# Pads in four SBUF pools of a hybrid streaming layer, and source order for its first twelve weight blocks

## The chip, the cores and the metric

The kernel runs on one core of one Trainium2 chip. The metric is the device time of one execution in microseconds (us); the median of the runs is what a change is judged by. On the core, TensorE does the matrix products into PSUM, VectorE (DVE), ScalarE (ACT) and GpSimd (POOL) do the work on vectors, SyncE (SP) issues most of the DMAs, and the DMA engines move data between HBM and SBUF. SBUF is the working memory: 128 partitions, and a tile takes the same range of bytes in each of them.

## The reference, cut to what matters

One layer of a streaming encoder over 384 tokens: 256 of a new prompt and 8 x 16 of running streams. All data is float32.

```python
h    = rmsnorm(x, norm_mix_g)                       # 384 x 2048
proj = h @ w_in                                     # columns: GLU | q | k | v | forget | gate A | gate B
u    = glu_in[..., :1024] * sigmoid(glu_in[..., 1024:])
z    = layernorm(causal_dwconv(concat(conv_buf, u), conv_dw_w, conv_dw_b), conv_ln_g, conv_ln_b)
a_out = (z * sigmoid(z)) @ conv_pw_out              # 1024 -> 2048
q, k = rmsnorm(q, q_norm_g), rmsnorm(k, k_norm_g)
logf = log_sigmoid(f_logit + b_forget)
b_out = attention(q, k, v, logf) @ w_att_out        # 1024 -> 2048
x    = x + (sigmoid(gA) * a_out + sigmoid(gB) * b_out) @ w_out
h2   = rmsnorm(x, norm_ffn_g)
up   = h2 @ w_up                                    # 2048 -> 2 x 5632
gc   = causal_dwconv(concat(ffn_buf, up[..., :5632]), ffn_dw_w, ffn_dw_b)
x    = x + (silu(gc) * up[..., 5632:]) @ w_down     # 5632 -> 2048
```

The kernel returns the two outputs x, the new keys, values and forget logits, and the last rows of both convolutions' inputs.

## The kernel before, in words

**Products.** Every float32 factor is split into a high part, rounded to the matrix engine's faster format, and a low part, the rest. A product is a trio of matmuls, one line of code each: high x high, high x low, low x high. Operands have 128 rows. In a job of kind "B" (lines 579 to 581, in the FFN lines 1807 to 1809) the *stationary* operand, which is loaded into the array ahead of the matmul, is a 128 x 128 piece of activations, and the *moving* one is a row of 512 (for V 344) weight columns. In a job of kind "A" (lines 574 to 576, the GLU columns) it is the other way round: the stationary operand is a piece of a weight tile, the moving one 384 tokens. The function `seven` (lines 618 to 620) does the Q columns with sums of tokens as further stationary operands (tiles `xsum0` to `xsum3`).

**Stages in the order of TensorE.** V columns, then Q, K, the rest of V, GLU columns beside the attention, gates A and B, then the attention's output projection (stationary tiles `aHL0`, `aHL1`) interleaved with the convolution's pointwise one (`zt0`, `zt1`), `w_out` (`mix0` to `mix3`), and the FFN (`xg`, `sums`, `late`, `x21h`/`x21l`, `act`). TensorE's instructions run in the order of the source.

**Weights.** The list `plan` holds all weight blocks of the kernel in the order of use; a block is 256 rows by 344 or 512 columns. `ahead` takes the next block off `plan` and calls `operand`: `fetch` issues its DMA on SP into one of three `raw` tiles, `split_rows` makes `hi` (ACT, line 408) and `lo` (DVE, line 409) in one of three pairs of tiles. So the load of a block waits until the `lo` of the third block before it is done. The first 16 blocks, here called b0 to b15, are those of V.

**x at the start.** `load_x` loads x by chunks of 128 features (lines 343 and 345, two DMAs for a chunk or a pair of them). `x_chunk` turns a chunk with three transposes on TensorE (line 696) and makes its high and low parts in the tiles `hT` (ACT line 700, DVE line 701). The generator `first_norm` calls it for chunks 2 to 15 between the V products and squares x for the norm on ACT (line 845). In the source, chunks 0 to 3 come first with b0 and b1, then pairs: 4 and 5 ahead of b3, 6 and 7 ahead of b5, and so on to 14 and 15 ahead of b13. `x_sums` and `token_sums` (lines 713 to 729) make `xsum` on ACT and DVE.

**What orders the queues.** The kernel is built three times. The first two builds give a class `Planner` the dependences, the places of the tiles and a cost for each instruction; it schedules greedily, always the ready instruction with the earliest due time on the engine that is free first, and the third build ties every instruction of ACT, DVE, SP and POOL ahead of the FFN to its predecessor in that schedule. A few rules are fixed in it: TensorE's order, the opening up to b1 (lines 734 to 764), the order of `log["chain"]`. The function `queued` marks an instruction as one of a chain in the order of the source on its engine. Before the change it puts the links of the chain into `log["chain"]` only where `banks` is filled, and that is in the FFN.

**Pools and places.** Tiles lie in pools that are stacked from both ends of the partition. From the left: `hi_lo` (3 `hi`, 3 `lo`, 4096 bytes each), `acts` (4 tiles of 12288 bytes), and on top of these, one after another, `x0` (x), `pair`, `convs`, `convs` with `attHL` on it, and `xg`. From the right, among others: `qkv`, and below it first `sums`, later `att`. Starts of the tiles from which stationary operands are read, in bytes of a partition, as the allocation of the kernel before has them:

| tiles | pool | first start | start modulo 128 | start modulo 512 |
|---|---|---|---|---|
| `hi`, `lo` (moving; stationary in GLU) | hi_lo | 2176 | 0 | 128 |
| `hT`, `mix`, `act`, `late` | acts | 26752 | 0 | 128 |
| `xsum0` | sums | 113760 | 96 | 96 |
| `hi`, `lo` of every fourth GLU block | att | 128992 | 96 | 480 |
| `aHL0` | attHL | 100704 | 96 | 352 |
| `zt0` | attHL | 125280 | 96 | 352 |
| `xg0`, `x21h`, `sums0` | xg | 75904, 116864, 125056 | 0 | 128 |

Each piece of such a tile that is loaded starts a multiple of 512 bytes further on.

Of the kernel before, what the change touches and what calls it, by code (L numbers as in the profile page):

```python
# [8 lines left out]
F32 = mybir.dt.float32  # L9
# [6 lines left out]
P = 128  # L16
# [18 lines left out]
TURN_AHEAD, PAIR_AHEAD = 100, 100  # L35
LAST_SUMS, SQ_WAIT = 8, 0

R_FFN, R_DWB, R_LNG, R_LNB, R_FDB, R_QG, R_N = 0, 16, 24, 32, 40, 84, 85
WARM, FILL = 5, 2

# [209 lines left out]
def hybrid_step(  # L250
# [12 lines left out]
    def pool(name, side="left", bufs=1, space=None):  # L263
        kw = dict(name=name, bufs=bufs, reuse_waits="tile")
        if space is not None:
            kw["space"] = space
        else:
            kw["side"] = side
        cm = tc.tile_pool(**kw)
        p = cm.__enter__()  # L270
        return p, lambda: cm.__exit__(None, None, None)

    cp, close_cp = pool("consts", side="right")
    rp, close_rp = pool("raw", side="right")
    wp, close_wp = pool("hi_lo")
    gp, close_gp = pool("acts")
    bank_pool, close_banks = pool("banks", space=PSUM)

    made = [-1, -1]
    banks, free = [], []  # L280
# [37 lines left out]
    xs = [p_x0.tile([P, NTT, 512], F32, name=f"xs{n}") for n in range(4)]  # L318
    xin = [x_prompt[0, 0:P, :], x_prompt[0, P:2 * P, :], x_sample.rearrange("b t d -> (b t) d")]

    newest = {}

    def kept(d):
        if order is None:
# [2 lines left out]
    def behind(ins, name):  # L327
        tc.add_manual_dep(ins, name, mybir.DependencyInfo(
            mybir.DependencyClass.NoSync, mybir.DependencyReason.DATA), reason="queue")

    def queued(d, chain=True):
        e = d.ins.engine
        if chain and e in newest:
            if banks or order is None:
                behind(d.ins, newest[e])
            if banks:
                log["chain"].append((newest[e], d.ins.name))
        newest[e] = d.ins.name

    def load_x(c, n):  # L340
        cs = slice(c * P, (c + n) * P)
        o = c % 4 * P
        queued(nc.sync.dma_start(xs[c // 4][:, 0:2, o:o + n * P],
                                 x_prompt[0, :, cs].rearrange("(t p) d -> p t d", p=P)))
        queued(nc.sync.dma_start(xs[c // 4][:, 2, o:o + n * P], xin[2][:, cs]))


    ident = cp.tile([P, P], F32, name="ident")
    nc.gpsimd.memset(ident[:], 0.0)
    queued(nc.gpsimd.affine_select(out=ident[:], in_=ident[:], pattern=[[-1, P]], compare_op=ALU.not_equal, fill=1.0,  # L350
                                   base=0, channel_multiplier=1))

# [60 lines left out]
        split_rows(hi, lo, raw, o, slice(0, 2))  # L413
        return hi, lo

    plan = []

    def planned(w, k0, cols, nk, *more):
        for k in range(k0, k0 + nk, 2):
# [62 lines left out]
    v_last = len(plan) - 16  # L482
# [192 lines left out]
    def drain(g):  # L675
        for _ in g:
            pass

    def job(kind, nk, act, evac, n=512, done=None):
        d = dict(kind=kind, nk=nk, act=act, evac=evac, n=n)  # L680
        if done is not None:
            d["done"] = done
        return d
# [101 lines left out]
    qt = p_qkv.tile([P, NTT, 1024], F32, name="qt")  # L785
    p_sm, close_sm = pool("sums", side="right")
    sums = [p_sm.tile([P, 2, 5, 2, P], F32R, tag=f"xsum{n}", bufs=1, name=f"xsum{n}") for n in range(4)]
    vrow = p_qkv.tile([P, P], F32, name="vrow")
    rows = [(norm_ffn_g, R_FFN, 16), (conv_dw_b, R_DWB, 8), (conv_ln_g, R_LNG, 8),
            (conv_ln_b, R_LNB, 8), (ffn_dw_b, R_FDB, 44), (q_norm_g, R_QG, 1)]  # L790
# [243 lines left out]
    p_cs, close_cs = pool("convs")  # L1034
# [3 lines left out]
    p_att, close_att = pool("att", side="right")  # L1038
# [141 lines left out]
    def glu_evac(g):  # L1180
        def ev(m, ps):
            if m < 2:
                sgb[m] = p_att.tile([P, NT], F32, tag="sgb", bufs=2, name="sgb")
                tt(sgb[m][:], ps[:, :NT], rs1b[:], op=ALU.mult)
                nc.scalar.activation(sgb[m][:], sgb[m][:], AF.Sigmoid)
            else:
                u = ut[:, 2 * g + m - 2, :]
                tt(u, ps[:, :NT], rs1b[:], op=ALU.mult)
                nc.gpsimd.tensor_tensor(u, u, sgb[m - 2][:], op=ALU.mult)
        return ev  # L1190

    sm = p_cs.tile([P, NT], F32, name="sm")
    sc = p_cs.tile([P, 8, 32], F32, name="sc")
    nc.gpsimd.memset(sc[:], 0.0)

    def conv():
        exts = {}
# [60 lines left out]
    att_steps = attention()  # L1258
    gemm([job("A", 16, ha, glu_evac(g)) for g in range(4)], [att_steps, conv_steps])
    drain(att_steps)  # L1260
    close_att()
    close_qkv()

# [826 lines left out]
```

## Time and profile before

| | |
|---|---|
| median of 3 runs | 1938.84 us (1938.63 to 1939.09) |
| the profiled execution | 1937.07 us, its span 1935.4 us |
| busy: TensorE, its weight loads | 1925.9 us, 1623.6 us |
| busy: DVE, ACT, POOL | 1609.7, 957.2, 153.2 us |
| granted TensorE clock | 1.000 |
| DMA | 293.37 MB, mean 152 GB/s |

The span runs from the first instruction of the program to the end of the last; the execution's own time has the launch around it. "Busy" is time in which at least one instruction of the engine is under way. Matmuls overlap each other, so a row's duration is not what a matmul adds to the time: that is the distance between the starts of neighbouring rows. A timeline lists instructions in the order of start: start, duration, engine, line, operation, output and inputs, shape, count, and in brackets the idle time ahead of it with what ended it. SPq is SyncE's queue, where a duration is the time that the DMA instruction took to be issued, waits included.

### The profile page before, as it was taken

The page shows a single profiled execution, that of the slowest core. Times are in us where ns is not written, and L with a number is a line of the kernel's source. Part 1 is how long each engine was busy: PE and PEld are TensorE (multiplying, and loading weights), DVE is VectorE, ACT ScalarE, POOL GpSimd, SP SyncE. Part 2 cuts the span into 40 slices and gives each one's busy share as a digit, 9 for nine tenths or more (in the row PEclk, how much of TensorE's full clock was granted, in tenths as well). Part 3 has the DMA queues.
Part 4 walks back from the last instruction along what each step waited for, and adds up shares of the span by engine and source line. Part 5 has one row for each costly group of instructions (what it writes and reads, how often), then busy time and mean ns, then how long its engine had stood idle before and what let it go on. Part 6 is the DMA issues. An engine that isn't in the chain of part 4 may idle for free.

```text
span 1935.4 us, 25489 instructions
## 1 busy us (share of the span) xinstructions
PE 1925.9 (100%) x9108; PEld 1623.6 (84%) x9108; DVE 1609.7 (83%) x2213; ACT 957.2 (49%) x1355; POOL 153.2 (8%) x298
## 2 busy tenths in 40 slices
PE   9999999999999999999999999999999999999999
PEld 8888999988888888888888888888888888888887
DVE  6878879998764568687699989899999999999985
ACT  7564444433333522354555464555555555555552
POOL 1000011100000000000101010101010101101010
PEclk9999999999999999999999999999999999999999
DMA  6547776344444333744545454545454545545453
GB/s 199 153 139 162 229 189 159 107 143 129 133 133 129 122 124 127 201 133 130 148 147 164 148 164 148 152 153 162 133 164 150 167 156 150 162 143 176 131 171 133
DMA packets 220722, 293.37 MB, mean 152 GB/s; under 512 B 59355, under 2 KB 105110, under 8 KB 220588
## 3 DMA queue, kind: packets, MB, share of 16 engines
q1 hardware_dynamic: 213395, 281.74, 49.0%
q0 software_dynamic: 7168, 10.00, 2.0%
q8 instruction: 71, 1.16, 0.2%
q14 instruction: 56, 0.45, 0.1%
q10 hardware_dynamic: 32, 0.01, 0.0%
HBM read 266.98 MB, written 7.86 MB: 142 GB/s over the span
## 4 chain that ended last, share of the span: by engine, by line
PE 98%; DMA 1%; ACT 0%; SPq 0%; DVE 0%; issue 0%; ACTq 0%
PE bank L1807 18%; PE bank L1808 18%; PE bank L1809 18%; PE bank L579 11%; PE bank L581 11%; PE bank L580 11%; PE bank L574 2%; PE bank L576 2%; PE bank L575 2%; PE bank L620 1%; PE bank L619 1%; PE bank L618 1%; DMA xs<-in_x_prompt_dram 1%; PE bank L1106 0%; PE bank L1147 0%; PE bank L1127 0%
## 5 line engine op out<-in xcount | busy, mean ns | idle before, releaser
L408 ACT CAST hi<-raw 128x1024 fp32r<-128x1024 f32 (+2 forms) x227 | 229.9, 1016 | 407.5 <-PE bank L581 256.1
L1499 ACT CAST hi<-raw 128x1024 fp32r<-128x1024 f32 x260 | 270.5, 1052 | 315.9 <-DVE raw L1499 140.2
L409 DVE TENSOR_TENSOR lo<-raw,hi 128x1024 fp32r<-128x1024 f32 (+2 forms) x227 | 268.1, 1184 | 158.6 <-ACT hi L408 157.0
L1499 DVE TENSOR_TENSOR lo<-raw,hi 128x1024 fp32r<-128x1024 f32 x260 | 314.1, 1218 | 49.0 <-ACT hi L1499 47.2
L579 PE MATMUL bank<-hi,hT 128*128 128x512 f32 (+1 forms) x624 | 235.6, 377 | 1.5 <-ACT hT L700 1.0
L580 PE MATMUL bank<-lo,hT 128*128 128x512 f32 (+1 forms) x624 | 232.8, 373 | 0.8 <-DVE lo L409 0.8
L581 PE MATMUL bank<-hi,hT 128*128 128x512 f32 (+1 forms) x624 | 233.3, 374 | 0.1
L1807 PE MATMUL bank<-hi,xg 128*128 128x512 f32 x440 | 171.2, 389 | 0.0
L1808 PE MATMUL bank<-lo,xg 128*128 128x512 f32 x440 | 171.2, 389 | 0.0
L1809 PE MATMUL bank<-hi,xg 128*128 128x512 f32 x440 | 171.2, 389 | 0.0
L1232 DVE SCALAR_TENSOR_TENSOR ut<-ext,cw,ut 128x384 f32<-128x384 f32 x240 | 151.7, 632 | 6.4
L1808 PE MATMUL bank<-lo,act 128*128 128x512 f32 x396 | 154.1, 389 | 0.0
L1809 PE MATMUL bank<-hi,act 128*128 128x512 f32 x396 | 154.0, 389 | 0.0
L1807 PE MATMUL bank<-hi,act 128*128 128x512 f32 x396 | 154.0, 389 | 0.0
L1499 ACT CAST x21h<-raw 128x1024 fp32r<-128x1024 f32 x82 | 86.4, 1054 | 102.9 <-PE bank L1809 52.7
L579 PEld LDWEIGHTS bank<-hi,hT 128*128 128x128 f32 x624 | 117.2, 188 | 21.1 <-ACT hT L700 1.5
L580 PEld LDWEIGHTS bank<-lo,hT 128*128 128x128 f32 x624 | 117.3, 188 | 20.0 <-DVE lo L409 1.3
L581 PEld LDWEIGHTS bank<-hi,hT 128*128 128x128 f32 x624 | 117.1, 188 | 19.9 <-DVE hT L701 0.9
L1499 DVE TENSOR_TENSOR x21l<-raw,x21h 128x1024 fp32r<-128x1024 f32 x82 | 100.2, 1222 | 6.6 <-ACT x21h L1499 5.6
L1809 PEld LDWEIGHTS bank<-hi,xg 128*128 128x128 f32 x440 | 82.6, 188 | 17.2
L1808 PEld LDWEIGHTS bank<-lo,xg 128*128 128x128 f32 x440 | 82.6, 188 | 17.1
L1807 PEld LDWEIGHTS bank<-hi,xg 128*128 128x128 f32 x440 | 82.6, 188 | 17.1
(397 smaller groups left out, 4139.7 us busy)
## 6 DMA issues: line engine op xcount, KB each, us to landing
raw<-in_w_up_dram SPq DMA_DIRECT2D x176, 512.0 KB
raw<-in_w_in_dram SPq DMA_DIRECT2D x96, 512.0 KB
raw<-in_w_down_dram SPq DMA_DIRECT2D x88, 512.0 KB
raw<-in_w_in_dram SPq DMA_DIRECT2D x64, 256.0 KB
raw<-in_w_out_dram SPq DMA_DIRECT2D x32, 512.0 KB
raw<-in_w_att_out_dram SPq DMA_DIRECT2D x16, 512.0 KB
raw<-in_conv_pw_out_dram SPq DMA_DIRECT2D x16, 512.0 KB
raw<-in_w_in_dram SPq DMA_DIRECT2D x23, 344.0 KB
```

Of the source, the lines that this page charges most:

```text
L408: queued(nc.scalar.copy(hi[:, k, :o], raw[:, k, :o]), first)
L409: queued(tt(lo[:, k, :o], raw[:, k, :o], f(hi[:, k, :o]), op=ALU.subtract), first)
L574: mm(o, hi[:, kk, s], ah, start=st, stop=False)
L575: mm(o, hi[:, kk, s], al, start=False, stop=False)
L579: mm(o, ah[:, s], hi[:, kk, :n], start=st, stop=False)
L580: mm(o, ah[:, s], lo[:, kk, :n], start=False, stop=False)
L581: mm(o, al[:, s], hi[:, kk, :n], start=False, stop=sp)
L1232: stt(o, v, wc, o, op0=ALU.mult, op1=ALU.add)
L1499: d = op(*args, **kw)
L1807: mm(o, ah, h[:, kk, :], start=start, stop=False, **kw)
L1808: mm(o, ah, l[:, kk, :], start=False, stop=False, **kw)
L1809: mm(o, al, h[:, kk, :], start=False, stop=stop, **kw)
```

## The change

Four small tiles that nothing uses are added: 384 bytes at the start of `hi_lo`, ahead of its other tiles, 96 bytes in `sums`, 32 bytes in `convs`, and 96 bytes in `att`. What lies left of a pad on a stack stays, what is stacked on it moves. With the sizes above the starts become: `hi` 2560, `hT` and `mix` and `act` 27136, `xg0` 76288, `x21h` 117248, `sums0` 125440 (multiples of 512 all); `xsum0` 113664 (a multiple of 512); `aHL0` 101120 and `zt0` 125696 (256 modulo 512); the `att` tiles `hi` 128896 (384 modulo 512). All are multiples of 128. `qkv` does not move: `vt`, stationary in a few attention products, stays at 154720, which is 96 modulo 128.

In `queued` the condition changes. With `plan` now made ahead of it, a link of the chain is made, and told to the planner, while `plan` is still empty, while at most b0 to b11 have been taken off it (`v_last` is its length less 16, and `EARLY` is 4), and in the FFN as before. So in the opening the DMAs of SP (and the splits and `hT` parts on ACT and DVE) that pass through `queued` keep the source's order among themselves up to b11; what does not pass through it there (squares, `x_sums`), and all later work, is placed by the planner.

```diff
+EARLY = 4
 ...
     wp, close_wp = pool("hi_lo")
+    wp.tile([P, 96], F32, name="align")
     gp, close_gp = pool("acts")
 ...
-    newest = {}
+    plan, newest = [], {}
 ...
     def queued(d, chain=True):
         e = d.ins.engine
         if chain and e in newest:
-            if banks or order is None:
+            if banks or not plan or len(plan) >= v_last + EARLY:
                 behind(d.ins, newest[e])
-            if banks:
                 log["chain"].append((newest[e], d.ins.name))
         newest[e] = d.ins.name
 ...
-    plan = []
 ...
     sums = [p_sm.tile([P, 2, 5, 2, P], F32R, tag=f"xsum{n}", bufs=1, name=f"xsum{n}") for n in range(4)]
+    p_sm.tile([P, 24], F32, name="align")
 ...
     nc.gpsimd.memset(sc[:], 0.0)
+    p_cs.tile([P, 8], F32, name="align")
 ...
     drain(att_steps)
+    p_att.tile([P, 24], F32, name="align")
     close_att()
```

## The prediction

> **What bounds the kernel now.** I read the page's busy times and its chain of work first, then the stretches of equal length, then single matmuls in the timeline.
>
> ```profile
> span 1935.4 us, 25489 instructions
> PE 1925.9 (100%) x9108; PEld 1623.6 (84%) x9108; DVE 1609.7 (83%) x2213; ACT 957.2 (49%) x1355; POOL 153.2 (8%) x298
> PE 98%; DMA 1%; ACT 0%; SPq 0%; DVE 0%; issue 0%; ACTq 0%
> ```
>
> TensorE is busy all but 9.5 us of the span, and the chain that ended last is 98% its own instructions. So the time is the number of matmuls times the distance of their starts, plus what little TensorE waits. "Busy" hides both, since overlapping matmuls count as busy whatever their distance. The stretches count matmuls in equal times (columns: stretch, length, then busy time and number for each engine, clock, DMA share, GB/s):
>
> ```profile
> 725.80:774.20 48.40, 48.40 (x209) 38.89 (x208) 41.22 (x58) 14.31 (x16) 0.00 (x0) 1.00 0.38 126
> 1209.60:1258.00 48.40, 48.40 (x215) 40.07 (x214) 42.77 (x56) 29.00 (x41) 9.55 (x19) 1.00 0.51 152
> ```
>
> The first lies mostly in the stage of attention output and pointwise projection, the second in the FFN. Both have trios with 512 moving columns at full clock, and TensorE sits idle in neither; yet one starts 209 in 48.4 us and the other 215. The timeline gives the distance:
>
> ```profile
> 116.18 0.39 PE L618 MATMUL bank<-hi,xsum 128*128 128x512 f32 x1
> 121.55 0.39 PE L620 MATMUL bank<-hi,xsum 128*128 128x512 f32 x1
> ...
> 650.21 0.40 PE L580 MATMUL bank<-lo,aHL 128*128 128x512 f32 x1
> 655.81 0.40 PE L580 MATMUL bank<-lo,aHL 128*128 128x512 f32 x1
> ...
> 1199.98 0.39 PE L1808 MATMUL bank<-x21l,xg 128*128 128x512 f32 x1
> 1205.42 0.39 PE L1808 MATMUL bank<-lo,xg 128*128 128x512 f32 x1
> ```
>
> Between the two rows of `xsum` lie 23 starts: 5.37 / 23 = 0.2335 us. Between those of `aHL` lie 24: 5.60 / 24 = 0.2333. Between those of `xg` lie 24: 5.44 / 24 = 0.2267. So a matmul with `xsum` or `aHL` stationary costs 6.6 ns more than one with `xg`. By the table of places the slow ones start at 96 modulo 128 and the fast one at 0; the region isn't the cause, since `xg`, `x21h` and `sums` lie in the same bytes as `aHL` and `xsum`.
>
> **The change: pads.** Each pad is an unused tile: no instruction and no DMA is added. These rows are of a grouping by line and shape (count, busy, mean ns):
>
> ```profile
> L579 PE MATMUL bank<-hi,aHL 128*128 128x512 f32 x96 | 37.9, 395 | 0.0
> L579 PE MATMUL bank<-hi,zt 128*128 128x512 f32 x96 | 37.9, 395 | 0.0
> L618 PE MATMUL bank<-hi,xsum 128*128 128x512 f32 x40 | 15.8, 394 | 0.0
> ```
>
> Each stands for a trio of three lines, so the slow matmuls are 3 x (96 + 96 + 40) = 696. At 6.6 ns they give back 696 x 0.0066 = 4.6 us: 3.8 in the projections, 0.8 in the Q stage. Nothing lies beside it: TensorE is the path, and what would be late next has room. DVE, which makes the weights' low parts, is busy 41.22 of 48.40 us in the projections' stretch and DMA has a share of 0.38 there; 3% more pace is covered.
>
> GLU has a test of its own: every fourth block there has its stationary weights in `att`, at 96 modulo 128, against 384 moving tokens.
>
> ```profile
> 212.36 0.33 PE L574 MATMUL bank<-hT,hi 128*128 128x384 f32 x1
> 220.71 0.34 PE L574 MATMUL bank<-hT,hi 128*128 128x384 f32 x1
> 224.88 0.35 PE L574 MATMUL bank<-hT,hi 128*128 128x384 f32 x1
> ```
>
> From 212.36 run two blocks at 0 modulo 128, 48 starts, 8.35 / 48 = 0.1740 us; from 220.71 the `att` block, 24 starts, 4.17 / 24 = 0.1738. No difference, so I take nothing for the 7 such blocks of GLU; were they to gain like the others it would be 168 x 6.6 ns = 1.1 us, the upper end. It also warns that I know the cost only where 512 columns move. For the attention's small products in `att` I take nothing either; no row has one of them at both places.
>
> The pad in `hi_lo` is harder. `hT`, `mix`, `act`, `xg` sit at 128 modulo 512 and already run at 0.2267; they move to multiples of 512, where no row of before has a stationary tile. `xsum` (96 modulo 512) and `aHL` (352) cost the same, and so do GLU's two places (128 and 480). In no pair does the place modulo 512 matter, so I take 0, and keep the two other possibilities as rivals.
>
> **The change: order.** The first 57 us hold the only waits of TensorE that are worth anything:
>
> ```profile
> 13.98 0.40 PE L579 MATMUL bank<-hi,hT 128*128 128x344 f32 x1
> ...
> 15.46 0.32 PE L581 MATMUL bank<-hi,hT 128*128 128x344 f32 x1
> 16.17 0.43 PE L579 MATMUL bank<-hi,hT 128*128 128x344 f32 x1 [0.39 <-ACT hT L700]
> ...
> 18.03 0.49 PE L696 MATMUL bank<-ident,xs 128*128 128x128 f32 x3
> 19.01 0.43 PE L579 MATMUL bank<-hi,hT 128*128 128x344 f32 x1 [0.49 <-ACT hi L408]
> 19.92 0.42 PE L580 MATMUL bank<-lo,hT 128*128 128x344 f32 x1 [0.48 <-DVE lo L409]
> ...
> 25.86 0.49 PE L696 MATMUL bank<-ident,xs 128*128 128x128 f32 x3
> 26.11 0.40 PE L579 MATMUL bank<-hi,hT 128*128 128x344 f32 x1
> 26.86 0.42 PE L580 MATMUL bank<-lo,hT 128*128 128x344 f32 x1 [0.34 <-DVE lo L409]
> ...
> 28.86 0.32 PE L581 MATMUL bank<-hi,hT 128*128 128x344 f32 x1
> 32.65 0.32 PE L581 MATMUL bank<-hi,hT 128*128 128x344 f32 x1
> ```
>
> Undisturbed, these start 3.79 / 24 = 0.158 us apart (the last two rows); the restart after a wait costs some 0.1 to 0.4 more. The wait before 16.17 is worth 1.0 us with its restart, those before 19.01 and 19.92 together 1.5 (the block b3), that before 26.86 0.7. Sum 3.2 us. Why, by ACT, DVE and SP's queue:
>
> ```profile
> 9.36 0.88 DVE L409 TENSOR_TENSOR lo<-raw,hi 128x688 fp32r<-128x688 f32 x1 [0.51 <-ACT hi L408]
> ...
> 9.70 0.77 ACT L408 CAST hi<-raw 128x688 fp32r<-128x688 f32 x1
> 14.93 0.63 ACT L845 ACTIVATE junk<-xs 128x512 f32<-128x512 f32 x1 [0.61 <-DMA xs<-in_x_prompt_dram]
> 15.56 0.56 ACT L700 ACTIVATE hT<-bank,gm 128x384 fp32r<-128x384 f32 x1
> 18.19 0.77 ACT L408 CAST hi<-raw 128x688 fp32r<-128x688 f32 x1 [0.99 <-DMA raw<-in_w_in_dram]
> ```
>
> ```profile
> 3.76 0.95 SPq L384 DMA_DIRECT2D raw<-in_w_in_dram  x2
> 4.75 0.47 SPq L343 DMA_DIRECT2D xs<-in_x_prompt_dram  x1
> ...
> 8.61 0.81 SPq L343 DMA_DIRECT2D xs<-in_x_prompt_dram  x1
> 11.77 0.37 SPq L384 DMA_DIRECT2D raw<-in_w_in_dram  x1
> 17.11 0.38 SPq L384 DMA_DIRECT2D raw<-in_w_in_dram  x1
> ```
>
> ```profile
> 12.00:18.00 6.00, 5.55 (x33) 4.66 (x32) 1.57 (x3) 4.56 (x13) 0.00 (x0) 1.00 0.97 353
> 30.00:36.00 6.00, 6.00 (x42) 5.97 (x42) 5.14 (x12) 5.21 (x12) 0.00 (x0) 1.00 0.61 178
> ```
>
> b3 is issued at 11.77 behind the x of chunks 2 to 9, lands only for the `hi` at 18.19, 6.4 us later, in a stretch where the DMA engines are 97% busy: it queues behind x that TensorE doesn't need yet. The `hT` at 15.56 stood behind a square at 14.93 that waited for x.
>
> In the source's order SP runs chunks 2 and 3, b2, chunks 4 and 5, b3, b4, chunks 6 and 7, b5. Of the moved DMAs: b2 goes behind one pair of chunks (256 features x 384 tokens x 4 bytes, 384 KB, 1.1 us at the 353 GB/s of the stretch from 12 us, 2 at half of that; its `hi` ran at 9.70 and its products start at 13.98, so it is covered). Four DMAs of chunks 6 to 9 go behind b3, that is 768 KB out of its way, 2.2 us at 353 GB/s; the planner may put the free pair 14 and 15 into that gap and take half of it back. b3's waits of 1.5 us should go either way, or nearly. b4 waits on SP for `lo` of b1 (9.36 to 10.24) rather than going out at 17.11, and the x of 6 and 7 queues behind that wait: issued near 11, wanted by TensorE at 25.86 (its chunk 6), and even 6.4 us of landing leaves 8. ACT and DVE stand in nearly the source's order already; the squares come later with their x, into 30 to 57, where ACT has room (5.21 of 6.00) and TensorE no wait.
>
> Bounds of this part: +3.2 us if all three waits go; below nothing, a new wait as large as the largest of these, -1.5. I take +1.5, b3's alone: the other two hang on ACT's order, which the planner makes anew. A gain here stays to the end, since after 57 us TensorE has no wait to fill up.
>
> **Sum.** 4.6 + 0 + 1.5 = 6.1 us. The profiled execution took 1937.07 us (span 1935.4 and 1.7 around it), so it would be 1931.0; it lies 1.8 under the median, and on the median of 1938.84 the forecast is 1932.7. Best case of the terms: 4.6 + 1.1 + 3.2 = 8.9, so 1929.9; worst, 4.6 - 1.5 = 3.1, so 1935.7.
>
> **Rivals.**
> - *The place modulo 128 is not what costs.* GLU's blocks speak for it, the two equal rates at 96 modulo 128 against it. Then only the order pays: 1938.84 - 1.5 = 1937.3, no change. [...] Chance 0.07.
> - *The order costs what the pads give.* An x pair or a block lands late behind SP's waits and TensorE loses more than 0.7 us where I expect a gain; with -1.5, 1935.7, no change by the bound below. Chance 0.05.
> - *Slower: a multiple of 512 is a worse place.* If the FFN's tiles took the step of 6.6 ns the wrong way, the 4,900 matmuls after 822 us (1,110 / 0.2267) would lose 32 us: 1965. It decides from 6.1 + 3.9 = 10 us, that is 2 ns each. Nothing speaks for it but that the place is untried. Chance 0.04.
> - *Much faster: a multiple of 512 is a better place.* The same step the right way gives 1938.8 - 6.1 - 32 = 1901. [...] Against it: nothing here varies with the place modulo 512. Chance 0.04.
>
> **How the numbers follow.** The forecast has 0.80. Runs of this kernel agree within 0.03%, but I call faster or slower only what differs by over 0.2%, 3.9 us. Faster: 0.80 and 0.04, 0.84. Same: 0.07 and 0.05, 0.12. Slower: 0.04. The range goes from 1928.8, the best sum with 1.1 more for the attention's products, to 1936.5, past the worst; it leaves out the two rivals of 512, the first rival, and a little of the forecast's tails.
>
> **What would show it.** Right: starts 0.2267 apart for `aHL`, `zt` and `xsum`, the projections' stretch with 215 instead of 209 matmuls, GLU and FFN unchanged; b3 on SP ahead of chunks 6 to 9, no idle time before its matmuls near 18 us. Wrong: 0.2333 again at the new places, another distance in the FFN, or new waits of TensorE on `hT` between 20 and 57 us.

## Result and profile after

| kernel | median | runs | ratio to before, 95% interval |
|---|---|---|---|
| before, timed beside it | 1938.89 us | 9 | |
| after | 1934.51 us | 9 | 0.9976 [0.9966, 0.9986] |

The change is worth 4.4 us, 2.7 to 6.6 by the interval; the lower end of that lies under the 3.9 us from which the prediction calls a change faster. All ratios are taken over undisturbed runs, which leaves out one run of `three_pads` (below) that took 3246.36 us at a granted clock of 0.556. The profiled execution of after took 1935.30 us with a span of 1933.5. The lines of its page that answer to those of before:

```profile
span 1933.5 us, 25489 instructions
PE 1923.6 (99%) x9108; PEld 1627.1 (84%) x9108; DVE 1608.8 (83%) x2213; ACT 956.3 (49%) x1355; POOL 154.5 (8%) x298
PE 99%; SPq 1%; DMA 0%; DVE 0%; issue 0%; ACT 0%
```

The instructions are as many as before, and TensorE is still the whole path; what changed can only be the distance of its starts or its few waits. The same two stretches as before, projections and FFN:

```profile
725.80:774.20 48.40, 48.40 (x215) 40.09 (x214) 42.08 (x60) 13.78 (x16) 0.00 (x0) 1.00 0.39 126
1209.60:1258.00 48.40, 48.40 (x215) 40.10 (x214) 43.67 (x56) 28.30 (x38) 9.58 (x19) 1.00 0.51 150
```

The first went from 209 matmuls to 215; the second kept its 215. DVE is busy 42.08 us of 48.40 in the faster one, so it had the room. The timeline of after, TensorE: the first matmul of Q, of GLU, of the projections and of `w_out`, with pairs of `xsum` and `aHL` between them.

```profile
62.97 0.39 PE L618 MATMUL bank<-hi,hT 128*128 128x512 f32 x1
...
117.42 0.39 PE L618 MATMUL bank<-hi,xsum 128*128 128x512 f32 x1
...
122.63 0.39 PE L620 MATMUL bank<-hi,xsum 128*128 128x512 f32 x1
...
214.18 0.34 PE L574 MATMUL bank<-hT,hi 128*128 128x384 f32 x1
...
643.53 0.39 PE L579 MATMUL bank<-hi,aHL 128*128 128x512 f32 x1
...
649.88 0.39 PE L580 MATMUL bank<-lo,aHL 128*128 128x512 f32 x1
...
655.32 0.39 PE L580 MATMUL bank<-lo,aHL 128*128 128x512 f32 x1
...
774.09 0.39 PE L579 MATMUL bank<-hi,mix 128*128 128x512 f32 x1
```

`aHL`: 5.44 / 24 = 0.2267 us from start to start, where before had 0.2333. `xsum`: 23 starts in 5.21 us, 0.2265. The stages, from these starts and the same ones of before (`w_out` first starts at 775.96 there):

| stage | before, us | after, us | difference |
|---|---|---|---|
| start to first Q | 60.98 | 62.97 | +1.99 |
| Q, K, rest of V | 151.38 | 151.21 | -0.17 |
| GLU, attention, gates | 429.21 | 429.35 | +0.14 |
| projections | 134.39 | 130.56 | -3.83 |
| `w_out`, FFN, to the end | 1159.40 | 1159.42 | +0.02 |

So the projections gave what they were to give, and the opening, where a gain was forecast, is longer. There SP's queue of after shows the order:

```profile
8.32 1.02 SPq L344 DMA_DIRECT2D xs<-in_x_prompt_dram  x1
9.38 0.47 SPq L346 DMA_DIRECT2D xs<-in_x_sample_dram  x1
9.89 0.38 SPq L935 DMA_DIRECT2D cwr<-in_conv_dw_w_dram  x1
10.32 1.48 SPq L938 DMA_DIRECT2D fwr<-in_ffn_dw_w_dram  x1
11.91 1.80 SPq L385 DMA_DIRECT2D raw<-in_w_in_dram  x1
13.75 2.41 SPq L933 DMA_DIRECT2D lp<-in_cache_logf_dram  x1
16.26 0.90 SPq L385 DMA_DIRECT2D raw<-in_w_in_dram  x1
17.21 0.47 SPq L344 DMA_DIRECT2D xs<-in_x_prompt_dram  x1
```

b3 is the `raw` at 11.91, b4 the one at 16.26. Chunks 6 and 7 (17.21) do stand behind b3 now, as the change orders. But ahead of b3 the planner has put x that it was free to move, that of chunks 14 and 15 (8.32, 9.38), and two small loads, `cwr` and `fwr`; `lp` stands ahead of b4. In before, the small loads came after b3 and b4:

```profile
19.04 0.41 SPq L934 DMA_DIRECT2D cwr<-in_conv_dw_w_dram  x1
19.49 0.45 SPq L937 DMA_DIRECT2D fwr<-in_ffn_dw_w_dram  x1
```

So b3 leaves SP no earlier than in before (11.77). Its `hi` runs 7.3 us later, where before had 6.4, and ACT and TensorE wait for it longer:

```profile
19.20 0.76 ACT L409 CAST hi<-raw 128x688 fp32r<-128x688 f32 x1 [2.79 <-DMA raw<-in_w_in_dram]
...
20.02 0.42 PE L579 MATMUL bank<-hi,hT 128*128 128x344 f32 x1 [2.11 <-ACT hi L409]
20.93 0.58 PE L580 MATMUL bank<-lo,hT 128*128 128x344 f32 x1 [0.49 <-DVE lo L410]
21.30 0.49 PE L581 MATMUL bank<-hi,hT 128*128 128x344 f32 x1
...
23.02 0.49 PE L581 MATMUL bank<-hi,hT 128*128 128x344 f32 x1
```

```profile
18.00:24.00 6.00, 3.49 (x13) 3.20 (x14) 2.86 (x5) 3.16 (x6) 0.00 (x0) 0.75 0.92 275
```

The wait for b3 is 2.11 us here against 0.49 in before. Behind it the granted clock was 0.75 over the stretch from 18 us (0.50 from 21.10 to 24.40), and the matmuls of 344 columns there start 1.72 / 6 = 0.287 us apart, where before had 0.158 at a clock of 1.00; these six alone cost 0.8 us more.

### The profile page after: what moved, and what is told of

It reads as the page before. It is cut to its first block, busy times and chain, and to the rows that moved or that the text cites. A ratio compares the mean times of both kernels' runs of the same rounds, so it can differ in the third digit from the quotient of the medians.

```text
span 1933.5 us, 25489 instructions
## 1 busy us (share of the span) xinstructions
PE 1923.6 (99%) x9108; PEld 1627.1 (84%) x9108; DVE 1608.8 (83%) x2213; ACT 956.3 (49%) x1355; POOL 154.5 (8%) x298
## 4 chain that ended last, share of the span: by engine, by line
PE 99%; SPq 1%; DMA 0%; DVE 0%; issue 0%; ACT 0%
PE bank L1811 18%; PE bank L1812 18%; PE bank L1810 18%; PE bank L580 11%; PE bank L579 11%; PE bank L581 11%; PE bank L574 2%; PE bank L576 2%; PE bank L575 2%; PE bank L619 1%; PE bank L620 1%; PE bank L618 1%; DMA raw<-in_w_in_dram 0%; PE bank L1107 0%; PE bank L696 0%; SPq L346 0%
```

## Experiments

Two questions were open: what each half of the change is worth, and whether "a multiple of 128" is what the pads buy. In all kernels the unchanged remainder is as in before or after.

**Each half alone.** `pads_only` is before with the four pads, `order_only` is before with the new condition in `queued` and no pad.

> The four pads on the kernel before, its planned order kept. Theory A (the pads give all of the gain, the order nothing or a loss): 4.6 us less than the kernel before, ratio 0.9976, at least as fast as the changed kernel; aHL, zt and xsum start 0.2267 us apart, the Q products begin near 61.0 us as before. Theory B (the order gives 1.5 us of the gain as forecast, the pads 3.1): ratio 0.9984, slower than the changed kernel by 1.5 us.

> The new condition in queued without any pad. Theory A: 0 to 2 us slower than the kernel before, ratio 1.000 to 1.001; b3 lands near 19 us behind x of chunks 14 and 15 and three small DMAs, TensorE waits 2 us for it, and the Q products begin near 63 us. Theory B: 1.5 us faster, ratio 0.9992, Q products begin near 59.5 us in undisturbed executions.

| kernel | median | ratio to before (1938.98 us) |
|---|---|---|
| pads_only | 1933.21 us | 0.9972 [0.9961, 0.9983] |
| order_only | 1940.15 us | 1.0010 [1.0001, 1.0019] |

The pads alone give 5.8 us by the medians, 3.3 to 7.6 by the interval. The order alone costs 1.2 (0.2 to 3.7). So the whole gain is the pads', and the order takes some of it back. Their stretch in the projections and that of the order alone, pads first:

```profile
725.80:774.20 48.40, 48.40 (x215) 40.10 (x214) 42.07 (x61) 14.23 (x16) 0.00 (x0) 1.00 0.40 131
```

```profile
725.80:774.20 48.40, 48.40 (x209) 38.89 (x208) 40.81 (x58) 13.64 (x16) 0.00 (x0) 1.00 0.39 125
```

And the timeline of `order_only`, ACT and TensorE:

```profile
19.83 0.77 ACT L408 CAST hi<-raw 128x688 fp32r<-128x688 f32 x1 [2.85 <-DMA raw<-in_w_in_dram]
...
20.65 0.42 PE L578 MATMUL bank<-hi,hT 128*128 128x344 f32 x1 [1.89 <-ACT hi L408]
```

The same late b3 as in after, without pads: it belongs to the order. Its granted clock stayed at 1.00 from 18 to 24 us, so the 0.75 of after is not a constant part of that wait.

**More blocks in the source's order.** `early0` is after with all 16 blocks of V, and so the x of chunks 14 and 15 too, in the source's order:

```diff
-EARLY = 4
+EARLY = 0
```

> The changed kernel with EARLY 0: all 16 blocks of V in the source's order, so x of chunks 14 and 15 go behind b12; cwr, fwr and lp still run ahead of b3. Theory A (what is put ahead of b3 is what delays it): 384 KB less ahead of b3, it lands 1 to 1.5 us earlier, near 17.5 to 18 us, TensorE's wait for it falls from 2.1 to under 1 us; 1 to 2 us faster than the changed kernel. Theory C (SP's own waits delay b3, whatever stands ahead): no change.

It took 1934.27 us, ratio 0.9975 [0.9966, 0.9984], no other than after: by the time theory C (SP's own waits) has it, and not theory A with its gain of 1 to 2 us. The rows say more. SP's queue, then ACT and TensorE:

```profile
6.78 0.51 SPq L935 DMA_DIRECT2D cwr<-in_conv_dw_w_dram  x1
7.34 1.24 SPq L938 DMA_DIRECT2D fwr<-in_ffn_dw_w_dram  x1
8.62 0.55 SPq L933 DMA_DIRECT2D lp<-in_cache_logf_dram  x1
9.29 6.19 SPq L385 DMA_DIRECT2D raw<-in_w_in_dram  x2
...
17.44 0.77 ACT L409 CAST hi<-raw 128x688 fp32r<-128x688 f32 x1 [2.74 <-DMA raw<-in_w_in_dram]
...
18.74 0.55 PE L696 MATMUL bank<-ident,xs 128*128 128x128 f32 x3 [1.32 <-ACT qt L713]
```

No x of chunks 14 and 15 stands ahead of b3 any more, but all three small loads do. b3 goes out at 9.29 and its `hi` runs at 17.44 instead of 19.20, about where theory A had it. TensorE still waits 1.32 us, for an ACT instruction that stands behind that `hi`. What is gained there is lost again at Q, where a wait of 1.04 us is new: with `EARLY = 0` the last squares of x are tied to the source's order too, which the next kernel shows.

**The small loads and the last x behind b3.** `late_small` is `early0` with a switch in `queued` that keeps the source's order for `lp`, `cwr` and `fwr` as well:

```diff
-    def queued(d, chain=True):
+    def queued(d, chain=True, late=False):
...
-            if banks or not plan or len(plan) >= v_last + EARLY:
+            if banks or late or not plan or len(plan) >= v_last + EARLY:
```

with `late=True` on the three loads.

> As EARLY 0, and cwr, fwr and lp chained in the source's order too, so that they go out behind the first Q blocks. Theory A: b3 is issued near 9 us, lands near 15, no wait of TensorE for it; Q products begin at 60 us or earlier; 2.5 to 3.5 us faster than the changed kernel, ratio to the kernel before 0.996. Theory C: as the changed kernel.

It took 1931.67 us, ratio 0.9965 [0.9953, 0.9978]. From its timeline:

```profile
8.20 1.66 SPq L385 DMA_DIRECT2D raw<-in_w_in_dram  x2
...
14.88 0.76 ACT L409 CAST hi<-raw 128x688 fp32r<-128x688 f32 x1
...
17.78 0.41 PE L579 MATMUL bank<-hi,hT 128*128 128x344 f32 x1
...
60.77 0.17 DVE L864 COPY rs<-r1r 128x3 f32<-128x3 f32 x1
...
61.05 0.57 DVE L895 TENSOR_SCALAR vt<-bank,rs 128x344 f32<-128x344 f32 x1
61.68 0.50 PE L618 MATMUL bank<-hi,hT 128*128 128x512 f32 x1 [1.03 <-DVE vt L895]
```

b3 goes out at 8.20 with no load ahead of it that isn't wanted first (the small ones follow from 52.85 us), its `hi` runs at 14.88 without a wait, TensorE has none for it at 17.78, and Q starts at 58.40 us instead of 62.97. But part of that is given back at once: the last squares of x run only at 52 to 55 us, the scale `rs` comes at 60.77, V's evacuation to `vt` waits for it, and TensorE waits 1.03 us for the bank. By the time alone `late_small` can't be told from `early0`, as their intervals overlap; that the small loads delay b3 is read from the rows.

**The squares free again.** `sp_only_late` is after (`EARLY` is 4) with `late=True` on the three loads and on both DMAs of `load_x`; SP's order is that of `late_small`, ACT's squares stay with the planner.

> The changed kernel, but the x of all chunks, lp, cwr and fwr always stand in the source's order on SP; ACT's squares keep the planner's order, which the kernel without any reordering of the small loads (the late_small kernel) had chained too. Theory: in late_small the wait of 1.4 us at the start of the Q stage came from the squares of the last group of chunks, chained to a late place on ACT, so that the scale of V's evacuation came late; with the squares free that wait goes and the early gain stays: Q starts near 58.4 us, no wait of TensorE over 0.5 us between 17 and 20 us or between 60 and 63 us, about 1930.4 us, ratio to the kernel before 0.996. Rival: the wait comes from x of chunks 14 and 15 themselves, which stand late on SP: then the wait near 60 us stays and the time is late_small's, 1931.7, ratio 0.9965.

It took 1931.18 us (1930.83 to 1931.45), ratio 0.9961 [0.9947, 0.9974] to a before of 1939.48. Its stretches:

```profile
18.00:24.00 6.00, 6.00 (x41) 5.96 (x40) 3.53 (x7) 5.76 (x12) 0.00 (x0) 1.00 0.77 217
57.00:63.00 6.00, 6.00 (x31) 5.20 (x30) 5.93 (x8) 5.25 (x8) 0.00 (x0) 1.00 0.31 94
```

TensorE is busy throughout in both: 41 matmuls lie between 18 and 24 us where after had 13, and the wait near 61 is gone. The squares run at 41 to 45 us here. Q starts at 58.45. The median is the lowest of all these kernels, 8.3 us (5.0 to 10.3) under before. But its interval overlaps with that of `late_small` and, by 0.0008, that of after, so that it is faster than they are rests on the rows.

**Is a multiple of 128 what counts?** `three_pads` leaves out the 384 bytes of `hi_lo`; `xsum` and the stationary tiles of the projections are at multiples of 128 in it all the same.

> The kernel before with three of the four pads: sums, convs and att, without the 384 bytes of hi_lo. The stationary tiles hT, mix, act, xg stay at 128 modulo 512, while aHL, zt and xsum are at multiples of 128. Theory (only the place modulo 128 counts): the same as all four pads alone, ratio 0.997, 1933 us, all matmuls of 512 columns 0.2267 us apart. Rival (a multiple of 512 is worth something, or hi_lo's pad moved something else): differs from the four pads by more than 2 us, and the FFN's distance is another than 0.2267.

```profile
116.59 0.40 PE L618 MATMUL bank<-hi,xsum 128*128 128x512 f32 x1
121.47 0.40 PE L618 MATMUL bank<-hi,xsum 128*128 128x512 f32 x1
725.80:774.20 48.40, 48.40 (x215) 40.10 (x214) 42.07 (x60) 14.04 (x16) 0.00 (x0) 1.00 0.36 125
```

1935.3 us, ratio 0.9977 [0.9968, 0.9986]: the time can't tell it from the four pads, the rows can. The projections run at 215 as expected. But `xsum`, at 113664, a multiple of 512, takes 21 starts in 4.88 us, 0.2324, and 0.233 on the mean of its matmuls: as slow as in before. So its own place isn't the cause. What differs from after, where the same `xsum` at the same 113664 ran at 0.2267, is the moving tile beside it: `hi` starts at 2176 here, and at 2560 in after. Modulo 256 the two tiles are 128 apart here and 0 apart in after.

**Shifting one side.** `acts_32` and `acts_64` are before with one unused tile of 32 or 64 bytes, so that nearly all stationary tiles move and `hi` and `lo` don't:

```diff
     gp, close_gp = pool("acts")
+    gp.tile([P, 8], F32, name="shift")      # 16 for acts_64
```

> The kernel before with an unused tile of 32 bytes at the start of the pool acts, nothing else. The stationary tiles hT, mix, act, xg, sums, late and x21 go from a multiple of 128 to 32 modulo 128, aHL and zt from 96 to a multiple of 128; xsum stays at 96; the weights' hi and lo keep their places. Theory (a stationary tile that isn't at a multiple of 128 costs 6.6 ns with 512 moving columns): 6,672 matmuls get slower and 576 faster, (6,672 - 576) x 0.0066 = +40 us, 1979 us; FFN starts 0.2333 us apart, aHL and zt 0.2267; V with 344 columns and GLU, whose moving tile hT is shifted here, show whether they pay too (4 us more if V's 432 matmuls and as much if GLU's 768 pay). Rival (something else at the place of xsum and aHL, a partner tile or the size of 96): FFN stays at 0.2267 and the time at 1939 or 1935.

> The kernel before with an unused tile of 64 bytes at the start of the pool acts, nothing else: hT, mix, act, xg, sums, late and x21 at 64 modulo 128, aHL and zt at 32, xsum at 96. If the step is at 64 bytes: FFN stays at 0.2267, aHL and zt at 0.2333, the time at 1939. If the step is at 128 bytes: FFN at 0.2333 too, +44 us, 1983. If the cost grows with the distance from a multiple of 128, FFN lies between or above, and aHL and zt at 32 below or above their 0.2333 at 96.

They took 1973.2 and 1976.3 us, a run each. The two stretches of `acts_32`, then of `acts_64`:

```profile
725.80:774.20 48.40, 48.40 (x215) 40.10 (x214) 37.63 (x53) 14.27 (x16) 0.00 (x0) 1.00 0.37 130
1209.60:1258.00 48.40, 48.40 (x210) 39.20 (x209) 41.69 (x49) 25.49 (x33) 6.91 (x14) 1.00 0.53 162
```

```profile
725.80:774.20 48.40, 48.40 (x209) 38.98 (x208) 36.51 (x51) 13.67 (x16) 0.00 (x0) 1.00 0.36 123
1209.60:1258.00 48.40, 48.40 (x210) 39.03 (x209) 43.52 (x53) 24.97 (x29) 5.63 (x11) 1.00 0.56 179
```

With 32 bytes the projections are cured (209 to 215) and the FFN is made ill (215 to 210). The totals were missed: +34 us in `acts_32` where +40 was expected, +37 in `acts_64` where +44 was expected for a step at 128 bytes. The expectations counted the 1,056 matmuls whose moving tile is `x21h` or `x21l`; those tiles moved by the same bytes as their partner and stayed near 0.2267 (in `acts_32` median 0.227, mean 0.2287). Without them it is (5,616 - 576) x 0.0066 = 33.3 for `acts_32` and 5,616 x 0.0066 = 37.1 for `acts_64`. The sums are thus another sign that the two places count together.

**The two theories against each other.** `all_32` shifts `hi`, `lo` and everything stacked on them by the same 32 bytes; `acts_128` shifts the stationary side by 128, so that each tile that was at a multiple of 128 still is; `sums_224` is `three_pads` with 224 bytes instead of 96 in `sums`, which puts `xsum` a multiple of 256 from `hi`.

```diff
     wp, close_wp = pool("hi_lo")
+    wp.tile([P, 8], F32, name="shift")      # all_32
     gp, close_gp = pool("acts")
+    gp.tile([P, 32], F32, name="shift")     # acts_128
```

> The kernel before with an unused tile of 32 bytes ahead of everything in the pool hi_lo: hi and lo, hT, mix, act, xg, sums, late and x21 all move by the same 32 bytes, to 32 modulo 128; aHL and zt come to a multiple of 128, and xsum stays at 96. Theory (what counts is the distance between the place of the stationary tile and that of the moving one, modulo 256): the FFN's distances are 0 as before, so 0.2267; aHL and zt keep their 224, so 0.2333 although they are at a multiple of 128; time of the kernel before, 1939 us. Rival (what counts is the stationary tile's own place modulo 128): FFN 0.2333 and 5,600 to 6,700 matmuls slower, +37 to +44 us, 1976 to 1983; aHL and zt 0.2267.

> The kernel before with an unused tile of 128 bytes at the start of the pool acts: hT, mix, act, xg, sums and late stay at multiples of 128, but at 128 modulo 256 from the weights' hi and lo. Theory (distance modulo 256): 6,672 matmuls less the 1,056 whose moving tile x21 moves along, 5,616 x 0.0066 = +37 us, 1976 us, FFN 0.2333 with hi and lo, 0.2267 with x21. Rival (a multiple of 128 is enough): no change, 1939 us, FFN 0.2267.

> The three pads of the kernel without hi_lo's pad, but 224 bytes instead of 96 in the pool sums, so that xsum lies a multiple of 256 from hi and lo. Theory (distance modulo 256): xsum 0.2267 instead of 0.2333, 0.8 us less than with 96 bytes, and the time of all four pads, 1933 to 1934 us, ratio 0.997. Rival: xsum stays at 0.2333 because hi_lo's pad brought the gain in another way; time of the three pads, 1935 us, ratio 0.9977.

The stretches of `all_32`, then of `acts_128`, and two rows of `xsum` in `sums_224`:

```profile
725.80:774.20 48.40, 48.40 (x209) 38.91 (x208) 41.21 (x59) 14.32 (x16) 0.00 (x0) 1.00 0.40 130
1209.60:1258.00 48.40, 48.40 (x216) 40.07 (x215) 42.28 (x55) 29.30 (x41) 9.54 (x19) 1.00 0.51 156
```

```profile
725.80:774.20 48.40, 48.40 (x208) 38.90 (x207) 36.35 (x50) 14.23 (x18) 0.00 (x0) 1.00 0.37 120
1209.60:1258.00 48.40, 48.40 (x210) 39.23 (x209) 43.60 (x52) 24.16 (x28) 5.64 (x11) 1.00 0.57 171
```

```profile
117.34 0.39 PE L618 MATMUL bank<-hi,xsum 128*128 128x512 f32 x1
122.10 0.39 PE L618 MATMUL bank<-hi,xsum 128*128 128x512 f32 x1
```

`all_32` took 1937.7 us (one run), the time of before: no FFN tile is at a multiple of 128, and it starts 216; `aHL` and `zt` are at a multiple of 128, and that stretch starts 209. `acts_128` took 1976.5 us (one run): every FFN tile is at a multiple of 128, and it starts 210. In `sums_224` 21 starts of `xsum` take 4.76 us, 0.2267; it took 1934.13 us, ratio 0.9974 [0.9964, 0.9984]. All three went by the distance of the two tiles, none by the stationary tile's own place. Collected, the means of the start-to-start times of the matmuls with 512 moving columns (starts more than 0.26 us apart left out; in the rows of `acts_...` also the 1,056 with `x21h` or `x21l`). The distance is the start of the stationary tile less that of the moving one:

| stationary and moving tile | kernel | distance modulo 256 | mean, us | matmuls |
|---|---|---|---|---|
| FFN and all others with `hi`/`lo` | before | 0 | 0.2268 | 6,619 |
| the same | all_32 | 0 | 0.2268 | 6,619 |
| the same | acts_32 | 32 | 0.2333 | 5,532 |
| the same | acts_64 | 64 | 0.2333 | 5,532 |
| the same | acts_128 | 128 | 0.2331 | 5,530 |
| `aHL`, `zt` | after, three_pads, acts_32 | 0 | 0.2267 | 575 each |
| `aHL`, `zt` | acts_64 | 32 | 0.2333 | 575 |
| `aHL`, `zt` | before, all_32 | 224 | 0.2333 | 575 each |
| `aHL`, `zt` | acts_128 | 96 | 0.2343 | 575 |
| `xsum` | before | 224 | 0.2334 | 103 |
| `xsum` | three_pads | 128 | 0.2331 | 103 |
| `xsum` | all_32 | 192 | 0.2294 | 103 |

Every distance of 0 in the table is fast. `aHL` in after lies 256 from its partner modulo 512 and ran at 0.2267, as fast as the FFN of before at 0 modulo 512 (0.2268). All others are slow; 192 alone lies between, and why isn't known. Distances that aren't a multiple of 32 weren't tried.

## Why the prediction came out, step by step

**The pads' sum** was forecast at 4.6 us, and `pads_only` measured 5.8 (3.3 to 7.6). The projections' 3.8 is exact: 576 matmuls, 134.39 to 130.56 us. The 0.8 in the Q stage is there too: the distances fall from 0.2334 to 0.2267 on 120 matmuls, and from the first Q start to the first of the remaining V matmuls after has 128.49 us where before had 129.30. That the whole stage is only 0.17 us shorter comes from these last 144 matmuls with 344 columns: their starts span 22.56 us in after and 21.93 in before. This isn't the pads' doing, since `early0` with the same pads has 21.93 too and `sums_224` 23.41; what moves it isn't known.

**The step that failed in it** is "the slow ones start at 96 modulo 128 and the fast one at 0", read as the cause. In before the two readings can't be told apart: `hi` and `lo` are at 128 modulo 256, and each fast tile happens to be as well. With this the next step fell too: "In no pair does the place modulo 512 matter, so I take 0" for the pad of `hi_lo`. It is worth the 0.8 us that the sum gave to `sums`, because only together do the two bring `xsum` and `hi` to one place modulo 256 (`three_pads`). The four pads do it all at once, so the total didn't show the error.

**GLU's `att` blocks** were taken at nothing, and the stage shows no gain: 429.21 and 429.35 us. It isn't quite nothing. These blocks lie at a distance of 96 in before, with a mean of 0.1735 from start to start, and at 128 in after, with 0.1759, where after's other blocks, at 0, have 0.1736. In `acts_128` it is the other way round: the blocks at 128 have 0.1758, those of `att`, at 224, 0.1737. So with 384 columns too a distance of 128 costs some 2 ns, and the pads together lose about 168 x 0.0024 = 0.4 us in GLU instead of buying anything. 0 and 96 (before), 32 and 192 (`acts_64`) and 224 (`acts_32`, `acts_128`) all have 0.1734 to 0.1742; 64, the distance of the `att` blocks in `acts_32` and in `all_32`, lies between (0.1745 in one, 0.1755 in the other).

**The order** was forecast at +1.5 us and is -1.2 by `order_only`, inside the bounds and on the wrong side. The step that failed: "Four DMAs of chunks 6 to 9 go behind b3, that is 768 KB out of its way". They did go, but SP's place ahead of b3 didn't stay empty. The working had the planner take half of it back with chunks 14 and 15; it took all of it, with them and with `cwr` and `fwr`, which the working didn't name, although the profile of before has them on the same queue. `late_small` shows it: with these kept behind, b3 leaves at 8.20 and its wait is gone. The three small loads alone count for much of it: with them ahead of b3 and no x, in `early0`, its `hi` ran at 17.44, without them at 14.88. The rival explanation, that b3 is held back by SP's own waits, falls with it: the blocks ahead of b3 are the same there.

**The rivals.** "The order costs what the pads give" came nearer than its chance of 0.05 says: a block did land late, and the order lost more than the 0.7 us that this rival asked for. That the total still fell by over 3.9 us is in part luck: the pads measured 5.8 us and not 4.6, a difference that lies within the noise, and that made up for the 1.2 that the order cost. A forecast of +4.6 for the pads and +1.5 for the order was thus met by the total with the cause of the one misread and the sign of the other wrong. The noise was underrated besides: the 0.03% by which runs agree is from three runs, and the nine of before beside after lie between 1936.93 and 1940.76, 0.2%, as much as the bound for a change. That the place modulo 128 isn't what costs was true, and its consequence, that the pads buy nothing, wasn't. The 32 bytes of `acts_32` cost 34 us, the same 32 bytes on both sides in `all_32` nothing. Both rivals of a multiple of 512 fell: the FFN runs 0.2267 in after as in before. Nor did any placing bring it under 0.2267.

**Opening times in one profile are weak evidence.** With the planner's old order Q started at 60.67 us in `pads_only`, 60.98 in before, 61.29 in `three_pads` and 62.89 in `sums_224`. So of the 1.99 us that the opening lost between the two profiles, only the 1.2 to 1.3 of the medians (`order_only` against before, after against `pads_only`) are put down to the order.

## What to carry to other kernels

Where the same kind of matmul starts at two distances at full clock (0.2267 and 0.2333 us here), compare the places of both its operands, not of the stationary one alone, and move one side, as `acts_32` did by 32 bytes, to see which relation holds before padding everything. Where a planner orders a queue, an order that is fixed for some loads frees slots for the others: list all that is still free to move on that queue, small loads too, and ask what will be set into the gap. And a gain of microseconds in the opening has to be followed to the next stage, where the late scale of V's evacuation took 1.5 us back in `late_small` (Q started as early as in `sp_only_late`, GLU at 210.54 instead of 209.02).

## What was not expected of the hardware

In these kernels a matmul with 512 moving float32r columns cost 0.2267 to 0.2268 us where its stationary and its moving tile lay at a distance of 0 modulo 256 bytes in the partition, and 0.2331 to 0.2334 at distances of 32, 64, 128 and 224, 0.2343 at 96 (0.2294 at 192, `xsum` of `all_32`): 3%, and 38 us of this kernel by one unused tile of 128 bytes (`acts_128`, 1976.5 to 1938.6). With 384 columns only the distance of 128 showed a clear step, a smaller one: 0.1758 to 0.1759 against 0.1734 to 0.1742. Why the distance matters isn't shown by these runs: in nearly all of them a matmul's stationary tile and that of the next lie at the same distance from the moving one, so it stays open whether its own loading of weights counts or the next one's.
